# Cross attention of a hybrid decoder layer: another order of the first head's products, scores among the last head's products, two PSUM banks for transposes and values spread over the steps

## The chip, the cores and the metric

The kernel runs on one core of a Trainium2 chip. A core has a matrix engine (TensorE, PE in the profile, with its weight loads as PEld), VectorE (DVE), ScalarE (ACT), GpSimd (POOL) and SyncE (SP, which here issues loads). Each engine works through its own list of instructions and is tied to the others by semaphores. The metric is the time of one execution on the device in microseconds (us), lower is better, as the median of three runs: 1311.14 us before, from 1310.99 to 1311.16.

## The reference, cut to what matters

One decoder layer of width 1024 on 1024 tokens, in float32: token mixing (gated linear attention beside a sliding window attention, with one output projection), cross attention into 256 memory tokens, and a gated MLP with a short causal convolution. All of the change lies in the cross attention:

```python
D_MODEL, SEQ, MEM_LEN, CROSS_HEADS, CROSS_DH = 1024, 1024, 256, 4, 256

def cross_attn(h, memn, w_q, w_k, w_v, w_o):
    B, T, _ = h.shape
    q = (h @ w_q).reshape(B, T, CROSS_HEADS, CROSS_DH)
    k = (memn @ w_k).reshape(B, MEM_LEN, CROSS_HEADS, CROSS_DH)
    v = (memn @ w_v).reshape(B, MEM_LEN, CROSS_HEADS, CROSS_DH)
    s = jnp.einsum('bqhd,bkhd->bhqk', q, k).astype(jnp.float32) * (CROSS_DH ** -0.5)
    p = jax.nn.softmax(s, axis=-1).astype(v.dtype)
    o = jnp.einsum('bhqk,bkhd->bqhd', p, v).reshape(B, T, D_MODEL)
    return o @ w_o

    # in the layer, after token mixing:
    h = h + cross_attn(rms_norm(h, norm_cross[l]), rms_norm(mem, norm_mem[l]), w_q_c[l], w_k_c[l], w_v_c[l], w_o_c[l])
```

k and v of all heads are made earlier in the program and lie in device memory.

## The kernel before, in words

**Numbers.** Every float32 operand of a matmul is split in two: `hi`, a cast by ACT to the matrix engine's own format (line 110), and `lo`, the float32 value less `hi`, by DVE (line 111). A product is then three matmuls, hi·hi, hi·lo and lo·hi, added up in a PSUM bank (`mm3`, lines 149 to 151, or the inner loop at line 1273). A matmul here is 128x512 (weights 128x128, 512 columns) or, in the scores, 128x256.

**Queries.** The q of one head (256 columns, 1024 tokens, depth 1024) is made by `query_pair` as a 2x2 block product with seven products in place of eight (Winograd's form of Strassen's): products 1 to 7, each of 4x3 matmuls, with sums of input blocks (`s1` to `s4` of the activations, from `query_sums` and `mix_out`; `w1` to `w4` of the weights, from `block_weights`) and sums of the results. Products 2, 7 and 3 go on adding in the bank of another product (2 in 1's, 7 in 6's, 3 in 5's), after that bank has been read. `v1`, `u2` and `u3` are SBUF tiles for the sums (lines 1276, 1280, 1282, 1262). The heads come in the order 2, 3, 0, 1; the first one (head 2) takes the products in the order 1276543, the others 1627543. The q of heads 2 and 3 goes to device memory (`q_d`) and comes back later (`reload`), since SBUF has no room. After head 2's products `cross_scales` makes the row scales of the softmax (with a matmul against ones, `psO<-ones,ss`). The PSUM banks have roles: F and S with three banks each, T and O with one each.

**Attention.** `scores(h, g)` is 12 matmuls of 128x256 into a bank S, for a group g of 256 queries (g from 0 to 3); `softmax` takes the maximum (DVE, line 1318), two exponentials with their sums (ACT, line 1323), a reciprocal and two scalings (DVE, lines 1325, 1327). `transposed(h, g)` turns the probabilities round with four matmuls into the bank T (line 1379), and ACT and DVE split them into `pt`. `values(h, n)` are 12 matmuls for each d of 0 and 1, for half the queries n, into banks F or S, and ACT copies the results out (line 1392). In `cross` the loop over h = 0, 1, 2 and g takes a transpose of head h, the scores of head h+1 and, at g = 2 and at the next head's g = 0, a whole `values`. Then come head 3's transposes and values among the first two columns of the output projection (`out_first`, plain products) and then the other columns as seven-product pairs (`out_pair`, from line 1529 on).

**What sets the order.** On the matrix engine the order is that of the code (`manual_schedule`). On DVE, ACT, POOL and SP the framework's scheduler sets the order, and pools of tiles with a few buffers each (`st` with 3, `w`, `sx` with 12, `kv` with 4, `pt` with 4, `cp` with 3, `c` with 3) set when a tile is free again. The loads are issued by SP in order; `kv` holds k and v of a head as the matmuls want them (512 KB a tile), and its slots lie over memory that the queries used before.

## Time and profile before

| what | value |
|---|---|
| time, median of three runs | 1311.14 us (1310.99 to 1311.16) |
| time of the profiled execution | 1310.63 us |
| its span in the trace | 1308.6 us |
| granted TensorE clock, mean | 0.998 |
| PE busy | 1280.2 us, 98% |
| DVE busy | 995.3 us, 76% |
| ACT busy | 634.3 us, 48% |
| first product of the first head on PE | 424.88 us |
| first product of `out_pair` on PE | 595.89 us |

Times within the trace are counted from the start of the span. In a row of the timeline the first number is the start, the second the duration; then come engine, line, operation, output and inputs by the program's names, the shape, and in brackets the idle time ahead with what ended it. A row of the waits names the engine and line that waited, what it waited for, the sum, the count and the longest. Of the 28 us in which PE was not busy over the whole span, 14.4 us are waits on other engines or loads between 420 and 660 us.

### The profile page before, as it was taken

The numbers are of one execution on the slowest core, as the hardware profiler recorded it, in microseconds if no ns is written. First come the engines' busy times: TensorE is split into PE (matmuls) and PEld (weight loads), VectorE is DVE, ScalarE is ACT, GpSimd is POOL, SyncE is SP. The second block draws the span as 40 slices with busy tenths as digits, with TensorE's granted clock in tenths as the row PEclk, the third lists the DMA queues.
The fourth block names the chain that finished last, engine by engine and source line by source line (L and its number), as shares of the span: only waits on it lengthen the run. The fifth ranks groups of instructions, "written<-read, shape, count | busy, mean of one in ns | idle before, by whom it ended". The sixth has DMA issues, their size and how long they took to land.

```text
span 1308.6 us, 17378 instructions
## 1 busy us (share of the span) xinstructions
PE 1280.2 (98%) x6503; PEld 1067.9 (82%) x6503; DVE 995.3 (76%) x1705; ACT 634.3 (48%) x1129; POOL 103.4 (8%) x181
## 2 busy tenths in 40 slices
PE   8999999999999999799999999999999999999997
PEld 8887777989888778778888888888888888888886
DVE  6849763378556976688689988888888886999687
ACT  5525545345444534674456534443444444454455
POOL 1400111101221000001100000000000000000001
PEclk9999999999999999999999999999999999999999
DMA  7642111249843443305422333232223138710204
GB/s 222 187 115 65 62 57 61 65 141 304 215 147 105 152 146 132 126 33 193 121 74 71 122 129 97 81 97 82 77 83 97 65 109 315 284 65 9 73 17 153
DMA packets 142363, 155.30 MB, mean 119 GB/s; under 512 B 16081, under 2 KB 108422, under 8 KB 142278
## 3 DMA queue, kind: packets, MB, share of 16 engines
q1 hardware_dynamic: 128822, 111.02, 27.4%
q0 software_dynamic: 13296, 42.91, 9.3%
q8 instruction: 51, 0.84, 0.3%
q14 instruction: 34, 0.28, 0.1%
q10 hardware_dynamic: 160, 0.27, 0.1%
HBM read 113.26 MB, written 42.48 MB: 119 GB/s over the span
## 4 chain that ended last, share of the span: by engine, by line
PE 94%; DVE 3%; ACT 1%; DMA 1%; issue 0%; SPq 0%; DVEq 0%; ACTq 0%
PE psS L1752 15%; PE psF L1752 13%; PE psF L149 8%; PE psF L150 8%; PE psF L151 8%; PE psF L1867 6%; PE psS L1867 6%; PE psS L1529 3%; PE psF L1273 3%; PE psS L151 2%; PE psS L150 2%; PE psS L149 2%; PE psO L1867 2%; PE psT L1867 2%; PE psS L1273 2%; PE psO L149 2%
## 5 line engine op out<-in xcount | busy, mean ns | idle before, releaser
L110 ACT CAST w<-st 128x1024 fp32r<-128x1024 f32 (+1 forms) x148 | 126.8, 860 | 212.2 <-PE psS L1867 39.6
L111 DVE TENSOR_TENSOR w<-st,w 128x1024 fp32r<-128x1024 f32 (+1 forms) x148 | 145.3, 984 | 46.1 <-ACT w L110 46.1
L1781 DVE SCALAR_TENSOR_TENSOR uy<-uy,vec,uy 128x1023 f32<-128x1023 f32 (+1 forms) x88 | 112.2, 1279 | 1.9 <-ACT uy L1779 1.5
L1867 PE MATMUL psF<-w,w 128*128 128x512 f32 x318 | 89.0, 389 | 0.0
L1867 PE MATMUL psS<-w,w 128*128 128x512 f32 x312 | 87.5, 389 | 0.0
L1752 PE MATMUL psS<-a,w 128*128 128x512 f32 x360 | 86.5, 389 | 0.0
L149 PE MATMUL psF<-xh,w 128*128 128x512 f32 x208 | 83.0, 399 | 0.0
L151 PE MATMUL psF<-xh,w 128*128 128x512 f32 x208 | 81.5, 392 | 0.0
L150 PE MATMUL psF<-xl,w 128*128 128x512 f32 x208 | 81.2, 390 | 0.0
L1752 PEld LDWEIGHTS psS<-a,w 128*128 128x128 f32 x360 | 67.6, 188 | 14.0
L1752 PE MATMUL psF<-a,w 128*128 128x512 f32 x324 | 77.8, 389 | 0.0
L1752 PEld LDWEIGHTS psF<-a,w 128*128 128x128 f32 x324 | 60.8, 188 | 12.6
L1867 PEld LDWEIGHTS psF<-w,w 128*128 128x128 f32 x318 | 59.7, 188 | 12.4
L1867 PEld LDWEIGHTS psS<-w,w 128*128 128x128 f32 x312 | 58.6, 188 | 12.1
L1779 ACT ACTIVATE uy<-uy,vec 128x1024 f32<-128x1024 f32 x44 | 54.7, 1247 | 18.6 <-DVE uy L1772 18.3
L1752 PE MATMUL psS<-act,wx 128*128 128x512 f32 x240 | 57.6, 389 | 0.0
L1752 PE MATMUL psS<-act,w 128*128 128x512 f32 x240 | 57.6, 389 | 0.0
L1752 PEld LDWEIGHTS psS<-act,w 128*128 128x128 f32 x240 | 45.1, 188 | 9.3
L1752 PEld LDWEIGHTS psS<-act,wx 128*128 128x128 f32 x240 | 45.0, 188 | 9.4
L1752 PE MATMUL psF<-act,wx 128*128 128x512 f32 x216 | 51.9, 389 | 0.0
L1752 PE MATMUL psF<-act,w 128*128 128x512 f32 x216 | 51.9, 389 | 0.0
L1033 ACT ACTIVATE prob<-prob,nm 128x256 f32<-128x256 f32 (+1 forms) x64 | 30.9, 484 | 39.8 <-DVE nm L1029 39.7
(530 smaller groups left out, 3137.9 us busy)
## 6 DMA issues: line engine op xcount, KB each, us to landing
st<-in_w_up_dram SPq DMA_DIRECT2D x44, 512.0 KB, 3.9
g_d<-uy POOLq DMA_DIRECT2D x22, 512.0 KB, 2.9
act<-in_w_down_dram SPq DMA_DIRECT2D x12, 512.0 KB, 10.3
st<-g_d SPq DMA_DIRECT2D x10, 512.0 KB, 3.9
res<-g_d SPq DMA_DIRECT2D x10, 512.0 KB, 9.1
st<-in_w_in_dram SPq DMA_DIRECT2D x9, 512.0 KB, 6.8
xt_d<-pts POOLq DMA_DIRECT2D x16, 256.0 KB, 5.1
ow_d<-pts POOLq DMA_DIRECT2D x32, 128.0 KB, 2.7
```

Of the source, the lines that this page charges most:

```text
L110: h = nc.scalar.copy(out=hi, in_=src)
L111: l = nc.vector.tensor_tensor(out=lo, in0=src, in1=hi.bitcast(F32), op=ALU.subtract)
L149: mm(out, lhsT=lh, rhs=rh, start=start, stop=False)
L150: mm(out, lhsT=lh, rhs=rl, start=False, stop=False)
L151: mm(out, lhsT=ll, rhs=rh, start=False, stop=stop)
L1033: last = nc.scalar.activation(out=prob[:, n, :nk], in_=prob[:, n, :nk], func=AF.Exp, bias=nm[:, n:n + 1], accum_out=den[:, n:n + 1])
L1273: mm(ps[n], lhsT=left[n][l][:, q], rhs=right[n][q][r], start=new and q == 0 and i == 0, stop=new and q == 3 and i == 2, skip_group_check=n ...
L1529: mm(ps, lhsT=left[n][l][:, q], rhs=right[n][q][r], start=new and q == 0 and i == 0, stop=new and q == 3 and i == 2, skip_group_check=not new)
L1752: nc.tensor.matmul(ps, lhsT=b[l][:, q], rhs=a[q][r], start=first and q == 0 and n == 0, stop=first and q == 3 and n == 2, skip_group_check ...
L1779: nc.scalar.activation(out=y, in_=u, func=AF.Identity, scale=self.v("cw2", j), bias=self.v("conv_b", j))
L1781: nc.vector.scalar_tensor_tensor(out=y[:, s:], in0=u[:, :T - s], scalar=self.v(nm, j), in1=y[:, s:], op0=ALU.mult, op1=ALU.add)
L1867: nc.tensor.matmul(ps[i], lhsT=g[:, l, tk], rhs=w[:, r], start=first and k == 0 and m == 0, stop=first and k == n - 1 and m == 2, skip_gro ...
```

## The change

It is confined to the cross attention; the number of matmuls stays.

1. **First head (head 2).** The product order becomes 1472563, with products 1, 4, 7 in banks F and 5, 6 in banks S; product 5's bank is copied to `u3` by ACT (one instruction more), and the sums that need 6 and 7 are made behind product 6. The other heads keep 1627543, all with banks F (head 3 had S).
2. **Sums of the first head.** `query_sums` is now a generator: the splits of s1, s2, s4 are written down one after each of the first products, with all their tiles taken at once. Head 2's `b22` lies in a tile of the pool that later holds head 0's k (`kt`), and its weights' sums t1, t4 come ahead of t2, t3. Head 0's k is loaded after head 2's products.
3. **First scores.** The scores and the softmax of head 0's groups 0, 1, 2 stand among head 1's products (behind 2, 5 and 3), no longer between head 0's products and head 1's.
4. **Transposes** take the banks T and O by turns. In the loop's first round the transposes of groups 0 and 1 stand close together with the last scores of head 0 between them.
5. **Values** are spread: each `values(h, n)` gives its d = 0 to one step and its d = 1 to the next, six matmuls each, behind the scores. Head 1 takes its groups in the order 2, 3, 0, 1.
6. **Loads and homes.** The `kv` loads go in the order v0, k1, v1, k2 and then q of heads 2 and 3 (before: k1, v0, q of head 2, v1, k2, q of head 3), so the tiles take other places.
7. **The end.** Head 3's transposes and values and the products of `out_first` are in another order, and one of its products goes to bank O.

```diff
     def query_sums(self, new):
-        for n, at, sl in (("s2", 0, slice(512, 1024)), ("s1", 4, slice(512, 1024)), ("s4", 4, slice(0, 512))):
+        tiles = {n: [[new("sx", [P, 2, 512], F32R, 12) for _ in range(2)] for _ in range(2)] for n in ("s2", "s1", "s4")}
+        for n, at, sl in (("s1", 4, slice(512, 1024)), ("s2", 0, slice(512, 1024)), ("s4", 4, slice(0, 512))):
             self.qa[n] = []
             for q in range(0, 4, 2):
-                hi, lo = (new("sx", [P, 2, 512], F32R, 12) for _ in range(2))
+                hi, lo = tiles[n][q // 2]
...
+            yield
...
             elif n == "6":
                 tt(out=u2, in0=ps[n], in1=v1, op=add)
                 if first:
-                    tt(out=u3, in0=ps["7"], in1=u2, op=add)
+                    tt(out=v1, in0=ps["7"], in1=u2, op=add)
+                    summed(1, t1, u3, v1, u3)
+                    summed(0, t1, ps["4"], v1, v1)
             elif n == "7" and not first:
                 tt(out=u3, in0=ps[n], in1=v1, op=add)
+            elif n == "5" and first:
+                nc.scalar.copy(out=u3, in_=ps[n])
...
+            next(between, None)
         return out
...
+        def first_scores():
+            yield
+            for g in range(3):
+                yield
+                probs[0, g] = self.softmax(self.scores(q[0], kt, g), g, cpnew)
+                yield
+
         for n, h in enumerate((2, 3, 0, 1)):
-            order = "1276543" if n == 0 else "1627543"
-            banks = dict(zip("14567", "FFSFF" if n == 0 else "SSSS" if n == 1 else "FFFF"))
-            ready = weights
-            q[h] = self.query_pair(ready, order, banks, tmp, o8)
+            order, banks = ("1472563", "14756") if n == 0 else ("1627543", "1654")
+            q[h] = self.query_pair(weights, order, dict(zip(banks, "FFFSS" if n == 0 else "FFFF")), tmp, o8,
+                                   sums if n == 0 else first_scores() if h == 1 else iter(()))
             if n < 3:
                 weights = self.query_weights((2, 3, 0, 1)[n + 1], new)
             if n == 0:
+                kt = self.memory_load(self.k_d[0], keep())
                 self.cross_scales()
...
-            if h == 0:
-                probs = {(0, g): self.softmax(self.scores(q[0], kt, g), g, cpnew) for g in range(3)}
...
-            pt = self.bank("T").rearrange("p (k q) -> p k q", k=2)
+            pt = self.bank("TO"[g % 2]).rearrange("p (k q) -> p k q", k=2)
...
-        def values(h, n, role):
+        def values(h, n, role, ds=(0, 1)):
...
+        def turn(h, i):
+
+            return (2, 3, 0, 1)[i] if h == 1 else i
+
...
+        memory_values(0)
         keys(1)
-        memory_values(0)
-        reload(2)
         memory_values(1)
         keys(2)
+        reload(2)
         reload(3)
...
-            for g in range(4):
-                transposed(h, g)
-                if h == g == 0:
+            for i in range(4):
+                if h or i != 1:
+                    transposed(h, turn(h, i))
+                if h == i == 0:
                     probs[0, 3] = self.softmax(self.scores(q[0], kts[0], 3), 3, cpnew)
-                score = self.scores(q[h + 1], kts[h + 1], g)
-                if g == 0 and h:
-                    values(h - 1, 1, "F")
+                    transposed(0, 1)
+                score = self.scores(q[h + 1], kts[h + 1], turn(h + 1, i))
+                if h:
+                    part = (h - 1, turn(h - 1, 2) // 2) if i < 2 else (h, turn(h, 0) // 2)
+                    values(*part, "F", (i % 2,))
+                elif i > 1:
+                    values(0, 0, "F", (i - 2,))
...
         transposed(3, 0)
-        values(2, 1, "F")
+        values(2, 1, "F", (0,))
+        steps(early, 1)
+        transposed(3, 1)
+        values(2, 1, "F", (1,))
+        steps(early, 3)
+        next(first)
+        transposed(3, 2)
+        values(3, 0, "S")
+        weights = self.out_weights(1, new)
+        next(weights)
+        marks = transposed(3, 3)
         steps(early, 2)
         next(first)
...
-                banks[c, h] = self.bank("F")
+                banks[c, h] = self.bank("O" if c == h == 1 else "F")
```

The line numbers of the changed kernel are 2 to 23 higher here (1276 is 1278, 1323 is 1330, 1379 is 1393, 1392 is 1406).

**ACT in the attention's loop, around the transposes of groups 2 and 3 of head 0 and group 0 of head 1** (`pt<-psT` or `psO` is the first half of a transpose's split, 1323 or 1330 the exponentials, 1392 or 1406 a copy of values). Before:

```order
377 L110 CAST pt_5061<-psT_5063 128x2x256
378 L1323 ACTIVATE cp_5054,cden_5055<-psS_5038,cmx_5051,rs_4468 128x256 x2
379 L1392 COPY o_5083<-psF_5085 128x512
380 L110 CAST act_5487<-o_5083 128x512
381 L1392 COPY o_5084<-psF_5093 128x512
382 L1323 ACTIVATE cp_5104,cden_5105<-psS_5070,cmx_5101,rs_4468 128x256 x2
383 L110 CAST pt_5061<-psT_5111 128x2x256
384 L110 CAST act_5487<-o_5084 128x512
385 L110 CAST pt_5141<-psT_5143 128x2x256
```

The changed kernel at the same place:

```order
378 L110 CAST pt_5061<-psT_5063 128x2x256
379 L1330 ACTIVATE cp_5054,cden_5055<-psS_5038,cmx_5051,rs_4468 128x256 x2
380 L1406 COPY o_5083<-psF_5085 128x512
381 L1330 ACTIVATE cp_5096,cden_5097<-psS_5070,cmx_5093,rs_4468 128x256 x2
382 L110 CAST pt_5061<-psO_5103 128x2x256
383 L110 CAST act_5487<-o_5083 128x512
384 L1406 COPY o_5084<-psF_5123 128x512
385 L110 CAST pt_5141<-psT_5143 128x2x256
```

Each transpose's cast still stands behind a copy or a pair of exponentials, but one in two of them now reads bank O, and one copy of values stands between two casts where two stood.

**DVE in the second head of the queries (head 3)**, around the read of product 6's bank (`c_4501<-ps…_4517`, `u2` and what frees the bank for product 7; `w_…` are low halves of weights; `rs_…` are row scales). Before:

```order
606 L111 TENSOR_TENSOR wx_4461<-st_4445,wx_4460 128x1024
607 L188 TENSOR_TENSOR rs_t_4481<-rs_y_4482 128x8
608 L111 TENSOR_TENSOR w_4465<-st_4444,w_4464 128x1024
609 L189 TENSOR_TENSOR rs_t_4481<-rs_t_4481,rs_v_4480 128x8
610 L190 TENSOR_SCALAR rs_t_4481<-rs_t_4481 128x8
611 L111 TENSOR_TENSOR w_4610<-st_4605,w_4609 128x1024
612 L191 TENSOR_TENSOR rstd_4479<-rs_y_4482,rs_t_4481 128x8
613 L1280 TENSOR_TENSOR c_4501<-psS_4517,c_4500 128x512
```

The changed kernel:

```order
606 L111 TENSOR_TENSOR w_4463<-st_4442,w_4462 128x1024
607 L183 TENSOR_SCALAR rs_v_4480<-psO_4470 128x8
608 L111 TENSOR_TENSOR w_4614<-st_4606,w_4613 128x512
609 L188 TENSOR_TENSOR rs_t_4481<-rs_y_4482 128x8
610 L111 TENSOR_TENSOR w_4610<-st_4605,w_4609 128x1024
611 L189 TENSOR_TENSOR rs_t_4481<-rs_t_4481,rs_v_4480 128x8
612 L1282 TENSOR_TENSOR c_4501<-psF_4517,c_4500 128x512
```

The read of the bank now stands behind a low half (`w_4614`, row 608) of the second weight tile (`st_4606`) of the head after, too.

**DVE at the end of the loop**, around the last two transposes of head 3 (`pt<-psT`, and in the changed kernel `psO`; line 1177 and `act`, `kv` are the output projection's operands). Before:

```order
762 L111 TENSOR_TENSOR act_5626<-o_5083,act_5625 128x512
763 L111 TENSOR_TENSOR act_5626<-o_5084,act_5625 128x512
764 L1177 TENSOR_TENSOR o_5423<-o_5423,o_5083 128x512
765 L1177 TENSOR_TENSOR o_5424<-o_5424,o_5084 128x512
766 L111 TENSOR_TENSOR pt_5597<-psT_5598,pt_5596 128x2x256
767 L111 TENSOR_TENSOR kv_5634<-o_5423,kv_5633 128x512
768 L111 TENSOR_TENSOR kv_5634<-o_5424,kv_5633 128x512
769 L111 TENSOR_TENSOR act_5660<-o_5578,act_5659 128x512
770 L111 TENSOR_TENSOR act_5660<-o_5579,act_5659 128x512
771 L111 TENSOR_TENSOR pt_5597<-psT_5652,pt_5596 128x2x256
```

The changed kernel:

```order
756 L111 TENSOR_TENSOR act_5610<-o_5245,act_5609 128x512
757 L111 TENSOR_TENSOR act_5610<-o_5246,act_5609 128x512
758 L111 TENSOR_TENSOR pt_5566<-psT_5567,pt_5565 128x2x256
759 L1177 TENSOR_TENSOR o_5083<-o_5423,o_5083 128x512
760 L1177 TENSOR_TENSOR o_5084<-o_5424,o_5084 128x512
761 L1177 TENSOR_TENSOR o_5423<-o_5083 128x512
762 L1177 TENSOR_TENSOR o_5424<-o_5084 128x512
763 L111 TENSOR_TENSOR pt_5566<-psO_5600,pt_5565 128x2x256
```

Both of the last transposes' low halves now stand eight rows earlier in DVE's list, and the last one ahead of the halves of `act` and `kv` that stood between the two.

More of the change, by code (lines that the diff above doesn't have):

```diff
@@ L1236, in query_sums, with query_weights, query_pair @@
                     self.qa[n].append((hi[:, i], lo[:, i]))
-    def query_weights(self, h, new):
+            yield
+    def query_weights(self, h, new, b22=None):
         def halves():
+            if b22 is not None:
+                return iter([b22[:, s].rearrange("p d m -> p (d m)").rearrange("p (k c) -> p k c", c=P)
+                             for s in range(2)])
             return iter([new("w2", [P, 4, P], F32R, 4) for _ in range(2)])
-        _, _, weights = self.block_weights(self.a["w_q_c"][0], 2 * h * P, (2 * h + 1) * P, new, halves)
+        _, _, weights = self.block_weights(self.a["w_q_c"][0], 2 * h * P, (2 * h + 1) * P, new, halves, b22 is not None)
         return weights
-    def query_pair(self, weights, order, banks, tmp, o8):
+    def query_pair(self, weights, order, banks, tmp, o8, between=iter(())):
         nc, mm = self.nc, self.nc.tensor.matmul
@@ L1251, in query_pair @@
         left = dict(zip("1234567", (b11, b21, b22, w4, w1, w2, w3)))
-        right = dict(zip("1234567", (self.qa[n] for n in ("a11", "a12", "s4", "a22", "s1", "s2", "s3"))))
+        right = dict(zip("1234567", ("a11", "a12", "s4", "a22", "s1", "s2", "s3")))
         out = [[o8("o8", dt=F32R, bufs=8) for _ in range(2)] for _ in range(2)]
@@ L1255, in query_pair @@
         v1, u2, u3 = (tmp("c", [P, 512], bufs=3) for _ in range(3))
-        ps, first = {}, order == "1276543"
+        ps, first = {}, order[1] == "4"
         def put(d, sl, src):
@@ L1265, in query_pair @@
         for n in order:
-            new = n in "1456" or (first and n == "7")
-            if new:
-                ps[n] = self.bank(banks[n])
-            else:
-                ps[n] = ps[{"2": "1", "7": "6", "3": "5"}[n]]
+            new = n in banks
+            ps[n] = self.bank(banks[n]) if new else ps[{"2": "1", "7": "6", "3": "5"}[n]]
             for q in range(4):
                 for i, (l, r) in enumerate(((0, 0), (0, 1), (1, 0))):
-                    mm(ps[n], lhsT=left[n][l][:, q], rhs=right[n][q][r], start=new and q == 0 and i == 0,
+                    mm(ps[n], lhsT=left[n][l][:, q], rhs=self.qa[right[n]][q][r], start=new and q == 0 and i == 0,
                        stop=new and q == 3 and i == 2, skip_group_check=not new)
@@ L1381, in transposed @@
             return self.split(pt, *(t[:, :, sl] for t in parts[h, g // 2]))
-        def values(h, n, role):
-            if n == 0:
+        def values(h, n, role, ds=(0, 1)):
+            if len(self.oc) == 2 * h:
                 self.oc += [o8("o8", bufs=8) for _ in range(2)]
-            pth, ptl = parts.pop((h, n))
-            for d in range(2):
+            pth, ptl = parts[h, n]
+            for d in ds:
                 ps = self.bank(role)
@@ L1418, in cross @@
                         keys(3)
-                if g == 2:
-                    values(h, 0, "F")
-                probs[h + 1, g] = self.softmax(score, g, cpnew)
-                if h == 2 and g:
+                probs[h + 1, turn(h + 1, i)] = self.softmax(score, turn(h + 1, i), cpnew)
+                if h == 2 and i:
                     steps(early, 1)
@@ L1425, in cross @@
         transposed(3, 0)
-        values(2, 1, "F")
+        values(2, 1, "F", (0,))
[9 more added lines that the diff above has]
+        marks = transposed(3, 3)
         steps(early, 2)
         next(first)
-        transposed(3, 1)
-        steps(early, 2)
-        next(first)
-        values(3, 0, "S")
-        transposed(3, 2)
-        weights = self.out_weights(1, new)
-        next(weights)
-        steps(early, 4)
-        next(first)
-        marks = transposed(3, 3)
         for _ in early:
@@ L1444, in cross @@
         late = late()
+        next(first)
         next(first)
@@ L2126, in run @@
             o8 = o8s.enter_context(self.pool("o8"))
+            heads = ExitStack()
+            kvnew = heads.enter_context(self.pool("kv0"))
             with self.pool("p3") as new:
```

23 lines of the change are left out of this document (11 added, 12 removed).

## The prediction

> **What bounds the kernel now.** The page's busy times come first, then what the matrix engine (PE) waits for from the first head's first product (424.88 us) to the first product of `out_pair` (595.89 us), the stretch in which its order changes.
>
> ```profile
> PE 1280.2 (98%) x6503; PEld 1067.9 (82%) x6503; DVE 995.3 (76%) x1705; ACT 634.3 (48%) x1129; POOL 103.4 (8%) x181
> ...
> PEclk9999999999999999999999999999999999999999
> ```
>
> ```profile
> PE psT L1379 <- DVE pt L111: 6.1, 4, 1.5
> PE psT L1379 <- DVE cmx L1319: 2.1, 1, 2.1
> PE psF L1273 <- ACT c L1276: 1.9, 1, 1.9
> PE psS L149 <- DMA kv<-k_d: 1.5, 1, 1.5
> PE psS L149 <- ACT o L110: 1.1, 1, 1.1
> PE psS L149 <- ACT pt L110: 0.7, 1, 0.7
> PE psS L1273 <- DVE c L1262: 0.6, 1, 0.6
> PE psS L151 <- DVE o L111: 0.2, 1, 0.2
> PE psS L150 <- DVE pt L111: 0.2, 1, 0.2
> ```
>
> PE is the bound: 98% busy at full clock, so only what PE stands still, or does, counts. The list holds 12 waits, 14.4 us in all, of the 28.4 that the span has over PE's busy time. The change removes no matmul, so its gain lies in these 14.4 us and in what they hide at their edges.
>
> The five waits at line 1379 are the largest part: a transpose waits for its PSUM bank T. One such turn, on three engines:
>
> ```profile
> 524.37 0.60 PE L1379 MATMUL psT<-ident,cp 128*128 128x128 f32 x4
> 524.73 0.36 PE L149 MATMUL psS<-kv,o 128*128 128x256 f32 x1
> ...
> 526.00 0.28 PE L150 MATMUL psS<-kv,o 128*128 128x256 f32 x1
> 526.12 0.28 PE L151 MATMUL psS<-kv,o 128*128 128x256 f32 x1
> 527.93 0.63 PE L1379 MATMUL psT<-ident,cp 128*128 128x128 f32 x4 [1.53 <-DVE pt L111]
> ```
>
> ```profile
> 525.05 0.57 ACT L1323 ACTIVATE cp<-psS,cmx,rs 128x256 f32<-128x256 f32 x1
> ...
> 526.15 0.59 ACT L110 CAST pt<-psT 128x512 fp32r<-128x512 f32 x1
> ```
>
> ```profile
> 527.10 0.68 DVE L111 TENSOR_TENSOR pt<-psT,pt 128x512 fp32r<-128x512 f32 x1
> ```
>
> Bank T is written at 524.37; ACT runs a softmax's exponentials first and reads the bank at 526.15, DVE subtracts at 527.10, and the next transpose starts at 527.93, 3.56 us after the one before. PE has only a transpose (0.36) and a score (to 526.24) between. The engine that is late is not full, as the windows of heads 1 and 2 of the loop show (PE, PEld, DVE, ACT, POOL busy, clock, DMA share, GB/s):
>
> ```profile
> 540.80:560.20 19.40, 15.40 (x105) 13.75 (x103) 15.27 (x37) 14.49 (x38) 0.00 (x0) 1.00 0.09 28
> 560.20:582.00 21.80, 19.76 (x93) 15.97 (x94) 20.08 (x37) 15.07 (x30) 0.00 (x0) 1.00 0.13 49
> ```
>
> DVE is busy for 15.27 of 19.40 us, then for 20.08 of 21.80: the first stretch is latency, the second is close to a throughput limit.
>
> **The price of a wait.** The last score matmul before the wait started at 526.12 and the one before it at 526.00: the pitch is 0.12 at a duration of 0.28, so the next could have started at 526.24. It started at 527.93, 1.69 us later, where the list counts 1.53. Each of the 12 waits thus costs some 0.16 more than listed, 1.9 in all: **16.3 us** is what they cost.
>
> A second way to the same number is the content of the stretch:
>
> ```profile
> 424.88 2.88 PE L1273 MATMUL psF<-act,w 128*128 128x512 f32 x12
> ...
> 435.42 2.89 PE L1273 MATMUL psF<-sx,wx 128*128 128x512 f32 x12
> 438.14 2.88 PE L1273 MATMUL psS<-sx,w 128*128 128x512 f32 x12
> ...
> 447.54 1.84 PE L223 MATMUL psO<-ones,ss 128*128 128x1 f32 x16
> ...
> 529.84 0.40 PE L149 MATMUL psF<-pt,kv 128*128 128x512 f32 x1
> ...
> 532.59 0.60 PE L1379 MATMUL psT<-ident,cp 128*128 128x128 f32 x4
> ...
> 595.89 3.11 PE L1529 MATMUL psS<-act,w 128*128 128x512 f32 x13
> ```
>
> A product takes 438.14 − 435.42 = 2.72, two half values 532.59 − 529.84 = 2.75, a score 1.51, a transpose 0.36, the scales 1.7. With 28 products (76.2), 16 scores (24.2), 16 transposes (5.8), 16 half values (22.0), the eight products of `out_first` (21.8), the scales and five matmuls of `out_pair` (1.1) that is 152.8 of 595.89 − 424.88 = 171.0. So 18.2 us is not content; the 1.9 beside the 16.3 are starts some 0.1 us late behind a semaphore, which stay.
>
> **The transposes** (two banks, values spread): a step of the loop is now a transpose, a score and a half of values, 0.36 + 1.51 + 1.375 = 3.25 us, and a bank is asked for again after two steps, 6.5 us, against the 3.56 it takes to come free. The 6.1 and 2.1 us and five edges go: 9.0. What hides the cycle is the other bank and the half of values in each step; with one bank and the steps even, 3.56 − 3.25 would be left, 0.3 a step. In the first round, with a score between the first two transposes and none of values, T is asked for again after 0.36 + 1.51 + 0.36 + 2 × 1.51 = 5.25. DVE must now keep up in the round h = 2.
>
> ```profile
> 433.45 1.22 DVE L111 TENSOR_TENSOR w<-st,w 128x1024 fp32r<-128x1024 f32 x1
> 434.58 3.09 DVE L111 TENSOR_TENSOR sx<-o,sx 128x512 fp32r<-128x512 f32 x5
> ```
>
> Five rows at 512 columns took 3.09, 0.60 apart; one at 1024 columns is followed after 1.13. From the round's first transpose to the last of head 3 DVE has 33 rows at 512 columns (19.8) and the small ones of five softmaxes (by estimate 3.6): 23.4 us, against 25.5 of PE, 92%. That is the tightest place.
>
> **The first head.**
>
> ```profile
> 429.65 3.03 PE L1273 MATMUL psF<-act,w 128*128 128x512 f32 x12 [1.89 <-ACT c L1276]
> ```
>
> ```profile
> 427.46 1.65 ACT L110 CAST sx<-o 128x512 fp32r<-128x512 f32 x3
> 429.02 0.57 ACT L1276 COPY c<-psF 128x512 f32<-128x512 f32 x1
> ```
>
> Product 2 waits until product 1's bank is copied, and the copy stands behind three casts though product 1 ended at 427.76. In the new order 4 and 7 stand between 1 and 2, in banks of their own, 5.4 us of cover; product 3 adds on in 5's bank behind product 6, 2.72 of cover for ACT's copy. The waits of 1.9 and of 0.6 (the list's row at 1273 on DVE `c`) go, with edges 2.8. New: product 4, second in the order, needs the last block (`a22`) at about 429.7, three matmuls before its end. ACT has two casts of weights in front of that block's scaling; with the pitches of the rows I get the last low half at 429.7: between 0 and 0.5, taken as 0.05. The sums s1, s2, s4 I get at 433.7, 436.1, 438.5, for needs at 435.8, 438.5, 441.2: 2 us of room, no wait.
>
> **The second head** (head 3) is where the new order of DVE can cost. Product 7 adds on in 6's bank once DVE has read it into `u2`.
>
> ```profile
> 451.94 0.37 SPq L1715 DMA_DIRECT2D st<-in_w_q_c_dram  x1
> ```
>
> ```profile
> 457.40 0.63 ACT L110 CAST w<-st 128x512 fp32r<-128x512 f32 x1 [3.61 <-DMA st<-in_w_q_c_dram]
> ```
>
> ```profile
> 455.04 0.69 DVE L1280 TENSOR_TENSOR c<-psS,c 128x512 f32<-128x512 f32 x1
> ```
>
> That read now stands behind a low half of a weight tile of the head after (row 608 of DVE's order). Its load is issued once its staging tile is free, by my walk of DVE's rows (1.13 at 1024 columns, 0.60 at 512) at 445.1, and took 5.4 us before (451.94 to 457.3): 450.5, then a cast (0.63), the halves (0.60 and 1.13) and the small rows, so `u2` is read by 453.2 to 454.8. Head 3's product 7 is due at 445.62 + 3 × 2.72 = 453.8, a wait of 0 to 1.0, or 1.6 if DVE comes late to it. I take 0.5.
>
> **Loads, first scores, the end.** The first row is a window while the loads run, at 399 GB/s.
>
> ```profile
> 514.80:516.80 2.00, 0.62 (x5) 0.65 (x6) 1.12 (x3) 0.73 (x3) 0.00 (x0) 1.00 1.00 399
> ```
>
> ```profile
> 512.81 0.34 SPq L1302 DMA_DIRECT2D kv<-k_d  x1
> ```
>
> ```profile
> 516.18 0.35 PE L149 MATMUL psS<-kv,o 128*128 128x256 f32 x1 [1.53 <-DMA kv<-k_d]
> ...
> 577.72 0.51 PE L149 MATMUL psS<-pt,kv 128*128 128x512 f32 x1 [0.67 <-ACT pt L110]
> ```
>
> k of head 1 is issued at 512.81, when the last product frees its slot, and used at 516.18: 3.4 us, and PE had a transpose and a score of work. Now v of head 0 goes first, into a slot that is free a product earlier; k still waits for the last product, behind which PE has the score of group 2, a transpose, a score and a transpose ahead of the score that needs it: 1.51 + 0.36 + 1.51 + 0.36 = 3.7 against 3.4. The wait goes (1.7 with its edge); 0 to 1.5 may be left if v0's transfer ahead of it slows it, and I take 0.05. The first scores stood straight behind head 0's products and waited for their last sums (1.1 + 0.2, with edges 1.6); among head 1's products they have at least three products of cover. At the end the 0.7 and 0.2 (1.2 with edges) go, but `values(3, 1)` comes some 3.1 us after its last transpose, where the bank cycle above is 3.4 to 3.6: 0.4 is left, between 0 and 0.9.
>
> **Sum.** 9.0 + 2.8 + 1.7 + 1.6 + 1.2 = 16.3 removed; 0.05 + 0.5 + 0.05 + 0.4 = 1.0 new: 15.3 gained. All behind 595.89 depends on `out_pair`'s start and PE's rows there have no gap, so it stays. The profiled execution took 1310.63 for a span of 1308.6, about 2.0 outside it, and lies 0.5 below the median of the runs, 1311.14. The span becomes 1293.3, the median **1295.8 us**. With no new wait and the late starts halved it is 1294; with every bound of a new wait at its upper end (0.5 + 1.6 + 1.5 + 0.9 = 4.5) 1299.3. The likeliest case's own range is 1293.3 to 1297.8.
>
> **The rivals.**
>
> *A: the followers become the bound.* What fell away on PE was slack for DVE and ACT, whose lists run in order: a low half that waits for its weights holds every later read of a bank. For it: `u2` above, the 92% of the round h = 2, and 20.08 of 21.80 us in the window. Against: the first window's 79%. The price, at twice what I took in each of three places (1.0 in head 3, 1.0 at the end) and 2 us where DVE, at 23.4 plus 10% for its semaphores, passes PE's 25.5: 4 us, 1299. [...]
>
> *B: the loads come late.* q of head 2 now queues behind four tiles of k and v. k of head 1 lands 3.4 us after the last product, and the last tile of q of head 2 is the sixth behind it, each 512 KB at 399 GB/s, 1.31 us: 3.4 + 6 × 1.31 = 11.3. It is needed after six scores, five transposes and two half values, 13.6. For a delay: k and v still wait for slots, in order on SP, so one late slot holds all behind it. If k of head 1 is 1.5 late and q 3, the time is 1300. Against: two microseconds of room.
>
> *C: no gain.* The waits are the throughput of ACT and DVE in the loop and only move. Then 9.0 comes back and the new waits reach their upper 4.5: 2.8 is left of the 16.3, 1308.3, and within 0.2% of 1311.14 as soon as one more wait of half a microsecond stays. Against: 79% of DVE in the window where most waits lie.
>
> *D: slower.* One mechanism: PE without pauses from 424 us on gets less clock. For it: nothing yet; the clock is 1.00 in all windows above and 9 tenths or more in all 40 slices. It decides from a mean clock of 1293.3 / 1308.6 = 0.988 for the whole span; at 0.97, 1293.3 / 0.97 + 2.5 = 1336. [...]
>
> **How the numbers follow.** Forecast 0.62, A 0.20, B 0.10, C 0.04, D 0.04. The range has to take in A's and B's lower halves: 1293 to 1301 holds nearly all of the forecast's case and most of A and B, 0.8 or a little more. About 0.2%, 2.6 us, is what a measurement here tells from no change: faster by more 0.92, within it 0.04, slower by more 0.04.
>
> **What would show it.** In the new profile: no wait at the transposes (the list's first two rows gone; if T's wait goes and O's comes, two banks weren't enough); the first head's products 2.72 apart from 424.88 to 443.9; in head 3 a wait of at most 1 us before product 7, released by DVE `c`; no wait for `kv<-k_d` over 0.3; the first `out_pair` product at 580 to 582; the clock at 1.00. A wait over 2 us anywhere in 424 to 582, or PE idle behind 582, would make the forecast wrong, as would a busy time of DVE in the round h = 2 over 24 us.

## The result and the profile after

The changed kernel takes 1292.91 us (median), against 1311.15 for the kernel before in the same session: a ratio of 0.9857, 95% interval 0.9837 to 0.9876. One of the changed kernel's four executions took 5808.45 us; the ratio compares the means without it, and the other three lie between 1292.56 and 1293.01. The change gains 18.2 us, 1.4%; 15.3 were forecast, and the time lies 0.1 us below the lower end of the range.

The page's busy times of the changed kernel, and all waits of PE over its whole span:

```profile
PE 1277.1 (99%) x6503; PEld 1067.9 (83%) x6503; DVE 993.5 (77%) x1705; ACT 633.1 (49%) x1130; POOL 103.4 (8%) x181
```

```profile
PE psO L260 <- DMA vrows<-in_norm_mix_dram: 3.2, 1, 3.2
PE psS L521 <- DMA gr<-in_x_dram: 1.2, 1, 1.2
PE psF L149 <- ACT w L113: 0.8, 1, 0.8
PE psS L1013 <- DVE mx L1022: 0.2, 1, 0.2
```

All four rows belong to the work ahead of the cross attention. Between 420 and 650 us the list is empty: the twelve waits of before are gone and none took their place. The matrix engine's timeline in the attention:

```profile
425.18 5.60 PE L1275 MATMUL psF<-act,w 128*128 128x512 f32 x24
430.62 2.88 PE L1275 MATMUL psF<-act,wx 128*128 128x512 f32 x12
...
444.22 1.84 PE L223 MATMUL psO<-ones,ss 128*128 128x1 f32 x16
...
507.49 0.60 PE L1393 MATMUL psT<-ident,cp 128*128 128x128 f32 x4
...
519.17 0.60 PE L1393 MATMUL psT<-ident,cp 128*128 128x128 f32 x4
...
522.44 0.60 PE L1393 MATMUL psO<-ident,cp 128*128 128x128 f32 x4
...
545.23 0.60 PE L1393 MATMUL psT<-ident,cp 128*128 128x128 f32 x4
...
577.07 4.24 PE L1552 MATMUL psS<-act,w 128*128 128x512 f32 x18
```

The first two products stand in one row of 24 matmuls without a gap, a step of the loop takes 522.44 − 519.17 = 3.27 us (3.25 forecast), and `out_pair` starts 577.07 − 425.18 = 151.9 us after the first product, where it took 171.0. The content that the prediction counted was 152.8 with five matmuls (1.1) that now stand behind this point: 151.7. The stretch is at its content.

**A ruler for the runs.** The time ahead of the first product differs from execution to execution by up to 2 us (423.5 to 425.5 us in the fourteen traces here, also between kernels whose work there is alike). So the parts are measured in the trace from the first product's start to the end of the span, which leaves that out: 1308.6 − 424.9 = 883.7 us before, 1290.8 − 425.2 = 865.6 us after, 18.1 us less. The changed kernel and the two variants of it without any wait there (e7 and e8 below) differ by 0.1 us on this ruler. Each kernel has one trace, though, and a load that lands late in it counts as a loss (e4 below).

### The profile page after: what moved, and what is told of

Its sections match the earlier page's. It is cut to its first block, busy times and chain, and to the rows that moved or that the text cites. A ratio compares the mean times of both kernels' runs of the same rounds, so it can differ in the third digit from the quotient of the medians.

```text
span 1290.8 us, 17377 instructions
## 1 busy us (share of the span) xinstructions
PE 1277.1 (99%) x6503; PEld 1067.9 (83%) x6503; DVE 993.5 (77%) x1705; ACT 633.1 (49%) x1130; POOL 103.4 (8%) x181
## 4 chain that ended last, share of the span: by engine, by line
PE 98%; ACT 1%; DVE 0%; DMA 0%; issue 0%; SPq 0%; ACTq 0%; DVEq 0%
PE psS L1775 15%; PE psF L1775 13%; PE psF L149 8%; PE psF L150 8%; PE psF L151 8%; PE psF L1890 6%; PE psS L1890 6%; PE psF L1275 5%; PE psS L1552 3%; PE psS L149 3%; PE psS L150 3%; PE psS L151 3%; PE psO L1890 2%; PE psT L1890 2%; PE psO L149 2%; PE psO L151 2%
## 5 line engine op out<-in xcount | busy, mean ns | idle before, releaser
L1804 DVE SCALAR_TENSOR_TENSOR uy<-uy,vec,uy 128x1023 f32<-128x1023 f32 (+1 forms) x88 | 112.0, 1278 | 1.9 <-ACT uy L1802 1.5
```

Source lines behind the costliest of these rows:

```text
L1804: nc.vector.scalar_tensor_tensor(out=y[:, s:], in0=u[:, :T - s], scalar=self.v(nm, j), in1=y[:, s:], op0=ALU.mult, op1=ALU.add)
```

## The experiments

| kernel | first product, us | span, us | first product to end, us | against | difference, us | time, us | ratio to before, 95% interval |
|---|---|---|---|---|---|---|---|
| before | 424.88 | 1308.6 | 883.69 | | | 1311.15 | |
| changed | 425.18 | 1290.8 | 865.59 | before | −18.10 | 1292.91 | 0.9857 [0.9837, 0.9876] |
| e1, one bank | 424.11 | 1292.0 | 867.90 | changed | +2.31 | 1294.41 | 0.9864 [0.9849, 0.9878] |
| e2, values whole | 425.31 | 1292.6 | 867.30 | changed | +1.71 | 1294.08 | 0.9861 [0.9847, 0.9876] |
| e3, both of these | 424.50 | 1299.5 | 874.99 | changed | +9.40 | 1301.63 | 0.9919 [0.9904, 0.9934] |
| e4, before with two banks | 425.47 | 1303.0 | 877.49 | before | −6.20 | 1303.46 | 0.9931 [0.9914, 0.9947] |
| e5, first head's old order | 423.90 | 1295.4 | 871.47 | changed | +5.88 | 1297.72 | 0.9898 [0.9881, 0.9914] |
| e6, first scores back | 424.99 | 1293.9 | 868.89 | changed | +3.30 | 1295.82 | 0.9880 [0.9865, 0.9895] |
| e7, old order of loads | 423.50 | 1289.1 | 865.65 | changed | +0.06 | 1291.97 | 0.9852 [0.9837, 0.9866] |
| e8, more work on DVE | 424.79 | 1290.4 | 865.66 | changed | +0.07 | 1291.91 | 0.9851 [0.9836, 0.9866] |
| e9, before with the new first head | 425.07 | 1305.1 | 880.02 | before | −3.67 | 1306.59 | 0.9967 [0.9954, 0.9980] |
| e12, old end | 424.48 | 1291.7 | 867.25 | changed | +1.66 | 1293.82 | 0.9868 [0.9852, 0.9885] |
| e10, longer wait | 423.96 | 1309.2 | 885.27 | before | +1.58 | 1311.27 | one run |
| e11, much longer wait | 424.82 | 1321.6 | 896.74 | before | +13.05 | 1323.63 | one run |

The kernels were measured in several sessions, in which the kernel before took 1311.15 (changed, e5 to e8), 1312.30 (e1 to e4) and 1311.30 us (e9 to e12). By their times alone e1, e2, e6 and e12 can't be told from the changed kernel, since their intervals overlap its own; what is said of them rests on the traces. The spans of e7 and e8 are 1.7 and 0.4 us shorter than that of the changed kernel, and their first products came 1.7 and 0.4 us earlier (423.50 and 424.79); on the ruler they are equal.

### Two banks or values spread: e1 to e4

```diff
# e1, on the changed kernel (e4 is the reverse, on the kernel before)
-            pt = self.bank("TO"[g % 2]).rearrange("p (k q) -> p k q", k=2)
+            pt = self.bank("T").rearrange("p (k q) -> p k q", k=2)
# e2, on the changed kernel; e3 is e1 and e2 together
-                if h:
-                    part = (h - 1, turn(h - 1, 2) // 2) if i < 2 else (h, turn(h, 0) // 2)
-                    values(*part, "F", (i % 2,))
-                elif i > 1:
-                    values(0, 0, "F", (i - 2,))
+                if h and i == 0:
+                    values(h - 1, turn(h - 1, 2) // 2, "F")
+                elif i == 2:
+                    values(h, turn(h, 0) // 2, "F")
...
-        values(2, 1, "F", (0,))
+        values(2, 1, "F")
         steps(early, 1)
         transposed(3, 1)
-        values(2, 1, "F", (1,))
```

> The changed kernel with one difference: all transposes go to bank T again, values stay spread. Theory S (the cycle of the bank is latency, and even steps alone nearly cover it): in the changed kernel's trace a transpose's bank was free 2.0 to 3.5 us after the transpose's start, and a step takes 3.25 us, so only the short gaps wait: 0.3 and 0.2 in head 1's round, about 1 at the first pair of transposes (1.87 us apart), 0.4 at head 3's first pair (1.82 apart); with edges +2 to +3 us, 1295 to 1296. Theory B (the second bank is the cure): the waits of before come back, five of 1.5 to 2.1 or more, +8 to +10 us, 1301 to 1303.

> The changed kernel with one difference: the values stand whole (12 matmuls) in one step, as before, two banks stay. Theory B (two banks are enough): a bank is asked for again after two steps, 6.5 us however the values are spread, so no wait comes back: 0 to +1 us, 1293 to 1294. Theory S (the spread is the cure): steps without values are 1.87 us and ACT and DVE have only that between two transposes, so waits of about 1 us at every second step, +4 to +6 us, 1297 to 1299.

> The changed kernel with both undone: one bank T and whole values. Both theories: the five waits at the transposes of before come back and one more at the first pair, 9 to 11 us, 1302 to 1304. A third theory, that the waits came from the old order of ACT and DVE and not from the bank, expects less than half of that, under 1297.

> The kernel before with one difference: transposes take banks T and O by turns. Theory B: the five waits at the transposes go, 8.2 listed and 9.0 to 9.8 with their edges: 1301.5 to 1302.5. Theory S: two banks without the spread only move the waits to the probabilities' scaling or to the scores, less than 5 us is gained: 1306 or more.

The two theories were put as if one edit were the cure. Each nearly is, by itself. With one bank and the values spread, 2.31 us are lost; two of its transposes, and the list's only row:

```profile
PE psT L1393 <- DVE pt L111: 0.7, 3, 0.3
```

```profile
519.22 0.63 PE L1393 MATMUL psT<-ident,cp 128*128 128x128 f32 x4 [0.25 <-DVE pt L111]
522.51 0.60 PE L1393 MATMUL psT<-ident,cp 128*128 128x128 f32 x4
526.06 0.63 PE L1393 MATMUL psT<-ident,cp 128*128 128x128 f32 x4
```

Steps of 3.29 and 3.55 us: the bank's cycle shows through at 3.55, the 3.56 that the prediction had read from one turn, and it took 0.2 to 0.5 us in six places. The list names three of them. The transpose at 526.06 is 0.3 us late and has no bracket: the matmul ahead of it hides 0.16 of that with its tail (its duration of 0.39 over a pitch of 0.23), and the 0.14 that is left is less than any wait in these lists.

With two banks and whole values the loop has no wait at all. The 1.71 us of e2 stand around one row, at the loop's end, where a whole `values` follows head 3's first transpose with no score between:

```profile
547.52 0.50 PE L150 MATMUL psF<-pt,kv 128*128 128x512 f32 x1 [1.25 <-DVE pt L111]
```

With neither, the waits of before are back, and one more (9.40 us):

```profile
PE psT L1393 <- DVE pt L111: 6.3, 5, 1.5
PE psT L1393 <- DVE cmx L1326: 2.0, 1, 2.0
```

So the two edits replace each other: alone the spread is worth 9.40 − 2.31 = 7.1 us, the second bank 9.40 − 1.71 = 7.7, both 9.4. On the kernel before (e4) the second bank took away all five waits, yet the trace shows only 6.2, for others came. Of these rows one wait of 0.6 was there before, and the largest new one stands at the same place as in e2:

```profile
PE psS L1273 <- DVE c L1262: 1.2, 2, 0.6
PE psF L150 <- DVE pt L111: 1.1, 1, 1.1
PE psF L1273 <- DVE o L111: 0.2, 1, 0.2
```

By the trace's parts the second bank brought 8.8 us from the loop's first transpose to head 3's first, about what the theory of the bank expected, and lost 1.5 behind that and 1.0 in the first two heads, far from the transposes. The wait of 0.2 lies in the first head, at product 4, which starts 0.2 us late in the kernel before too, without a row. The second wait of 0.6 lies in the second head, where DVE's rows stand in the order of before, but a load of weights landed 1.0 us later. DVE's row behind that load, before and in e4:

```profile
457.40 0.69 DVE L1728 TENSOR_TENSOR st<-st,st 128x512 f32<-128x512 f32 x1 [1.52 <-DMA st<-in_w_q_c_dram]
```

```profile
459.08 0.69 DVE L1728 TENSOR_TENSOR st<-st,st 128x512 f32<-128x512 f32 x1 [2.54 <-DMA st<-in_w_q_c_dram]
```

Whether this belongs to e4 or to this one execution is not shown; the traced execution took 1304.99 us, the other three 1302.81 to 1303.79. The 6.2 is thus a lower value, and nearer 7 without the late load. Of the theories, neither "spread alone" nor "bank alone" stands for the whole kernel; the bank's cycle does.

### The first head's products: e5 and e9

```diff
# e5, on the changed kernel
-        for n, at, sl in (("s1", 4, slice(512, 1024)), ("s2", 0, slice(512, 1024)), ("s4", 4, slice(0, 512))):
+        for n, at, sl in (("s2", 0, slice(512, 1024)), ("s1", 4, slice(512, 1024)), ("s4", 4, slice(0, 512))):
...
                 if first:
-                    tt(out=v1, in0=ps["7"], in1=u2, op=add)
-                    summed(1, t1, u3, v1, u3)
-                    summed(0, t1, ps["4"], v1, v1)
+                    tt(out=u3, in0=ps["7"], in1=u2, op=add)
...
-            order, banks = ("1472563", "14756") if n == 0 else ("1627543", "1654")
+            order, banks = ("1276543", "17654") if n == 0 else ("1627543", "1654")
...
# e9: the changed kernel with cross() of before, out_first's old banks, and the first scores behind head 0's products
```

> The changed kernel with one difference: the first head's products in the order 1276543 again, with the old banks, sums and order of the splits. The prediction's term: the waits of 1.9 and 0.6 come back, 2.8 with their edges: 1295.5 to 1296. If the splits of the sums, which are now written in one after another, were the larger help, the old waits would not come back in full: under +1.5.

> The kernel before with the first two parts of the change alone (order and banks of the first head's products, its sums and its weights' homes, head 0's k loaded later); scores, transposes, values, loads and the end are as before. The prediction's term: the waits of 1.9 and 0.6 go, 2.8 with edges: from the first product to the end 883.69 - 2.8 = 880.9 us in the trace. If the two waits undone in the changed kernel (5.9 us there) are the measure, 877.8. If the second head's wait for `u2` exists in this surrounding, 881.4.

The old order in the new surroundings (e5) cost 5.88 us, twice the forecast. PE's row of the second product, and windows around it (PE, PEld, DVE, ACT, POOL busy, granted clock, DMA share, GB/s):

```profile
430.15 4.60 PE L1275 MATMUL psF<-act,w 128*128 128x512 f32 x12 [3.36 <-ACT c L1278]
```

```profile
427.00:431.50 4.50, 1.35 (x4) 1.14 (x5) 4.50 (x9) 4.50 (x10) 0.00 (x0) 0.91 0.40 117
431.50:434.00 2.50, 2.50 (x7) 1.95 (x6) 2.50 (x6) 2.50 (x6) 0.00 (x0) 0.50 0.00 0
434.00:437.00 3.00, 3.00 (x14) 2.41 (x14) 3.00 (x6) 1.37 (x3) 0.00 (x0) 0.98 0.00 0
```

Two things are in it. The wait for ACT's copy is 3.36 us and not 1.89, since ACT's list now has three casts of weights (423.88, 424.84 and 428.48 us) between the first product's start and that copy, where the kernel before has none; the new order had been covering that as well. And behind the wait the granted clock is 0.50 (in the window of 2.5 us above, and for 3.4 us in all): the product takes 4.60 us for 2.88. Undoing a part is thus not the same as the part by itself. By itself, on the kernel before (e9), the new first head is worth 3.67 us, 0.9 over the forecast. The waits at its products are gone, and from the first product to the matmul of the scales it takes 19.04 us where it took 22.66, 3.62 less. PE's wait for k of head 1 (1.5) is gone too, as its home was free early (issued at 501.09), but a transpose two steps on now waits in its place, so that this exchange is worth next to nothing:

```profile
516.15 0.66 PE L1388 MATMUL psT<-ident,cp 128*128 128x128 f32 x4 [1.40 <-DVE pt L111]
```

### First scores and loads: e6 and e7

```diff
# e6, on the changed kernel
...
-                                   sums if n == 0 else first_scores() if h == 1 else iter(()))
+                                   sums if n == 0 else iter(()))
...
+            if h == 0:
+                probs = {(0, g): self.softmax(self.scores(q[0], kt, g), g, cpnew) for g in range(3)}
# e7, on the changed kernel
-        memory_values(0)
         keys(1)
+        memory_values(0)
+        reload(2)
         memory_values(1)
         keys(2)
-        reload(2)
         reload(3)
```

> The changed kernel with one difference: the first three scores stand between head 0's and head 1's products again. Both theories: the waits on ACT and DVE `o` come back, 1.3 listed, 1.6 with edges. Theory K (the wait for k of head 1 went because a score now stands behind the last product): k is issued at the last product's end, lands 3.4 us later, and PE has 0.36 + 1.51 + 0.36 = 2.2 ahead of it: 1.2 more, in all +3 us, 1295.5 to 1296.5. Theory L (it went because of the order of the loads): +1.6 alone, 1294.5.

> The changed kernel with one difference: k and v and the reloaded q in the old order (k1, v0, q of head 2, v1, k2, q of head 3), and with it other homes. Theory K: no wait comes back, within 0.3 of the changed kernel, 1292.6 to 1293.2. Theory L: the wait for k of head 1 comes back, +1.5 to +1.8, 1294.5.

Both came out as theory K had it. With the scores put back, PE waits for ACT and DVE and, 27 us later, for the load again; with the loads put back, for nothing:

```profile
PE psS L149 <- DMA kv<-k_d: 1.2, 1, 1.2
PE psS L149 <- ACT o L110: 1.1, 1, 1.1
PE psS L151 <- DVE o L111: 0.2, 1, 0.2
```

The 1.2 us is what the sum of 3.4 (landing) less 2.2 (work ahead) had given. In the new order of loads the score that moved behind the last product is the load's cover. The old order is worth as much (0.06 us), but it does not need that cover: in e7 k of head 1 gets the home that is free early and is issued at 494.72 (506.02 in the changed kernel), as in e9, where the wait went without the score. So e7 does not show that the homes have no weight.

### DVE full, and PE not waiting: e8

```diff
-        nc.vector.tensor_reduce(out=mx, in_=ps, axis=mybir.AxisListType.X, op=ALU.max)
+        for _ in range(1 + more):     # more is 1 for the scores of head 3, 0 elsewhere
+            nc.vector.tensor_reduce(out=mx, in_=ps, axis=mybir.AxisListType.X, op=ALU.max)
...
```

> The changed kernel with four more maxima on DVE (each written twice, the same result), one per group of the loop's round h = 2, 0.60 us each, 2.4 us. DVE is busy for 22.35 of 22.63 us there and 22.24 of 22.24 us in the stretch behind. Theory bound (rival A of the prediction): PE waits for what is added, +1.5 to +2.5 us, 1294.5 to 1295.5. Theory slack (DVE works ahead there on operands of the output projection that are needed later): 0 to +0.5 us, 1293 to 1293.5.

The window of the round h = 2, first of the changed kernel, then of e8:

```profile
532.20:554.83 22.63, 22.63 (x138) 19.72 (x137) 22.35 (x52) 20.32 (x49) 0.00 (x0) 1.00 0.06 22
```

```profile
532.20:554.83 22.63, 22.63 (x139) 19.72 (x137) 22.49 (x53) 19.52 (x47) 0.00 (x0) 1.00 0.05 19
```

DVE is busy for 99% of the round in both, and 2.4 us of additional work cost 0.07. Part of what fills DVE there, 6.4 us in the changed kernel, are low halves for the output projection (`act`), which are wanted later: ten such rows stand in its window and eight in that of e8, so the added maxima pushed some of them back, and PE did not wait. Rival A read the share of busy time as nearness to a limit, and that falls.

### The end: e12

The edit puts the text from `first = self.out_first(...)` to the end of `cross` back, with product (1, 1) in bank F.

> The changed kernel with one difference: from head 3's first transpose on (transposes, last values, products of `out_first`, banks) the old order. The prediction's term: the waits of 0.7 and 0.2 come back, 1.2 with edges: from the first product to the end 865.59 + 1.2 = 866.8 us. The rest of the 18.1 us that the other undone parts leave (18.1 - 9.4 - 3.3 - 2.8 to 3.1 = 2.3 to 2.6) would make it 868.

It cost 1.66 us, between the two numbers. PE's rows at head 3's first values:

```profile
560.91 0.50 PE L149 MATMUL psS<-pt,kv 128*128 128x512 f32 x1 [0.68 <-ACT pt L110]
561.68 0.50 PE L150 MATMUL psS<-pt,kv 128*128 128x512 f32 x1 [0.27 <-DVE pt L111]
```

**The parts, added up.** Transposes 9.40 (e3), first head 3.67 (e9), first scores 3.30 (e6), loads 0.06 (e7), end 1.66 (e12): 18.09 us, where the whole change measured 18.10. That it closes to 0.01 is luck. e3 holds a wait of 0.2 at the first pair of transposes that the kernel before does not have, e6 has 1.2 for k's load where before has 1.5, and with the first head's 5.88 of e5 in place of the 3.67 of e9 the sum would be 20.3. So the first head's part depends on what stands around it, as the two halves of the first part (e1, e2) do on one another.

The two traces give the parts without any experiment. These rows are of the kernel before:

```profile
447.54 1.84 PE L223 MATMUL psO<-ones,ss 128*128 128x1 f32 x16
...
512.61 0.60 PE L1379 MATMUL psT<-ident,cp 128*128 128x128 f32 x4
...
561.34 0.63 PE L1379 MATMUL psT<-ident,cp 128*128 128x128 f32 x4 [1.53 <-DVE pt L111]
```

From the first product to the scales the change gains 3.62 us, from there to the first transpose 1.80, from that to head 3's first transpose 10.99, from there to `out_pair` 1.58 (the five matmuls counted alike) and behind it 0.11.

### What a longer wait costs: e10 and e11

```diff
# on the kernel before; 3 in e10, 5 in e11
             if n == "1":
-                nc.scalar.copy(out=v1, in_=ps[n])
+                for _ in range(3 if first else 1):
+                    nc.scalar.copy(out=v1, in_=ps[n])
```

> The kernel before with ACT's copy of the first head's product 1 written three times, so that PE's wait of 1.9 us there becomes 2.9. If only a stall as long as 3.4 us brings the clock down (as in the kernel with the first head's old order), the time from the first product to the end grows by 1.0 us and no more, the product behind the wait takes 3.0 us. If every stall beyond the 2.1 us that the kernel before had does, it grows by 2.5 and the granted clock behind the wait is about 0.5.

> The kernel before with the same copy written five times: a wait of 4 to 6 us (two casts come in between). If a stall over 3.4 us halves the granted clock for some 3.4 us, the next 8 or so matmuls take 0.63 us and the time grows by the added wait and 1.4 to 1.7 us on top; if the drop in the other kernel came from something else there, by the added wait alone.

e10 has the wait, 3.12 us, and the drop, which one of the two expectations allowed only at 3.4 us:

```profile
429.97 4.61 PE L1273 MATMUL psF<-act,w 128*128 128x512 f32 x12 [3.12 <-ACT c L1277]
```

```profile
427.00:429.00 2.00, 0.00 (x0) 0.00 (x0) 2.00 (x5) 1.97 (x5) 0.00 (x0) 1.00 0.19 41
429.00:431.00 2.00, 1.03 (x3) 0.82 (x4) 2.00 (x5) 1.93 (x4) 0.00 (x0) 0.87 0.65 231
431.00:433.00 2.00, 2.00 (x6) 1.61 (x5) 2.00 (x3) 1.99 (x3) 0.00 (x0) 0.50 0.00 0
433.00:435.00 2.00, 2.00 (x8) 1.60 (x8) 2.00 (x4) 0.39 (x1) 0.00 (x0) 0.78 0.54 147
```

The product takes 4.61 us where it took 3.03. Of the added 1.2 + 1.6 us 1.4 are left at the end of the first head, since the wait of 0.6 and the late starts there were absorbed; 0.18 more were lost at k's load, 1.58 in all. In e11 the wait was 10.19 us where 4 to 6 were expected, since the last two copies came behind other casts (433.75 and 437.25 us). The clock was 0.50 from 430.0 until 443.7 us, and it fell twice more, at 563.1 and 573.4 us, behind these waits:

```profile
562.62 0.63 PE L1380 MATMUL psT<-ident,cp 128*128 128x128 f32 x4 [2.08 <-DVE cmx L1320]
...
572.72 0.63 PE L1380 MATMUL psT<-ident,cp 128*128 128x128 f32 x4 [1.88 <-DVE pt L111]
```

The 13.05 us that e11 lost are 9.58 in the first head, 1.89 at the first and 1.59 at the second of these drops. The first of the two is the wait of 2.1 us that the kernel before has too, without a drop there. Why it drops the clock in one trace and not in the other is read from the traces in the last section.

## Why the prediction was right or wrong

**The bound and the mechanism: right.** The matrix engine's waits between 424 and 596 us were the gain, all twelve of them. The second way to the number, content against the stretch's length, gave 18.2 us of which 18.1 were gained. The sum went by the first way, and came out 2.8 us too low: `out_pair` started at 577.07, ahead of the 580 to 582 named as a sign. That the time lies only 0.1 us below the range is due to the range's lower end, which allowed for the case that no new wait comes and half of the late starts go; no new wait came, and nearly all of the late starts went.

**The step that failed is the price of a wait**, "Each of the 12 waits thus costs some 0.16 more than listed, 1.9 in all", with the sentence on the starts "which stay". Listed 14.4, gained 18.1: the list was short by 3.7 us and not by 1.9, 0.31 per wait on average. The experiments give the same order with other waits: e12 lists 0.95 in two waits and costs 1.66 (0.36 each over the list), e6 2.5 in three and 3.30 (0.26 each), e3 8.3 in six and 9.40 (0.18 each, transposes). The 0.16 is the tail of the matmul ahead (0.28 us over a pitch of 0.12).

Part of what was left out stands in a row that the prediction quotes: the product behind the wait of 1.89 took 3.03 us and one without a wait 2.88. The second matmul behind a wait starts late once more, by some 0.1 us at a product or a score (behind the wait that ended at 489.01 it comes at 489.23, 0.22 us later, where the others of that score stand 0.12 apart) and 0.03 at a transpose (0.63 us where one without a wait takes 0.60); with seven waits of the one kind and five of the other that is by estimate 0.8 us. Another part are late starts that the list does not have at all, as product 4 of the first head, in the kernel before:

```profile
441.09 3.01 PE L1273 MATMUL psF<-act,w 128*128 128x512 f32 x12
```

It stands 2.95 us behind product 5 (438.14), where the pitch is 2.72, and has no bracket. So the first head, with 2.5 us listed, held 3.62 us that went: it is the term most under its size, 2.8 in the sum. So the starts did not stay: 1.8 of their 1.9 us went with the waits. About half of that is traced to rows here, the rest is not.

**The four new waits, 1.0 together: none came.** Each was set at a value between its bounds, and no wait shows for any of them in the changed kernel.

```profile
452.67 0.69 DVE L1282 TENSOR_TENSOR c<-psF,c 128x512 f32<-128x512 f32 x1
...
556.67 0.68 DVE L111 TENSOR_TENSOR pt<-psO,pt 128x512 fp32r<-128x512 f32 x1
```

```profile
454.18 2.88 PE L1275 MATMUL psF<-act,wx 128*128 128x512 f32 x12
...
554.83 0.60 PE L1393 MATMUL psO<-ident,cp 128*128 128x128 f32 x4
...
558.03 0.39 PE L149 MATMUL psS<-pt,kv 128*128 128x512 f32 x1
```

`u2` was read by 453.36, 0.8 us ahead of product 7 (0.5 had been charged). The load behind it was issued at 445.30 and cast at 449.42, so it landed within 4.1 us; the 5.4 of before were taken over from a moment with more transfers (a DMA share of 1.02 from 451.94 to 457.30 us there; here 0.26 in the first 1.7 us of the load and 0.75 from 445.30 to 449.42). The last transpose's low half was done at 557.35, 0.7 us ahead of `values(3, 1)`: 2.5 us after the transpose, not the 3.4 to 3.6 of the loop's cycle, since DVE had only four rows of line 1177 (2.4 us) ahead of it and no softmax. The late block `a22` came in time, and so did k of head 1, with next to nothing to spare: it was issued at 506.02 and used at 509.71, 3.7 us later, which is also what it took in e6, where PE waited for it (509.07 to 512.79).

**Term by term**, by the experiments: transposes 9.0 forecast, 9.40 measured; first head 2.8 and 3.67; first scores with k's load 1.6 + 1.7 = 3.3 and 3.30; end 1.2 and 1.66; new waits −1.0 and 0. The differences are 0.4 + 0.9 + 0 + 0.5 + 1.0 = 2.8 us. By the two traces they are first head 0.8, first scores 0.2, transposes with k's load 0.3 (10.7 and 10.99), end 0.4, behind `out_pair` 0.1 and new waits 1.0, again 2.8.

**The rivals.** A (DVE becomes the bound): DVE did become full, 22.35 of 22.63 us, more than the 92% forecast (23.4 of 25.5, so the sum for PE was 2.9 us too long), and e8 shows that this was no bound. That the lists run in order shows at the first head's copy of before, which started behind three casts at 429.02, 1.3 us after its bank was done (427.76); the 10% for semaphores in this rival's price was the author's estimate, and no run shows it. B (late loads): no load came late; k of head 1 needs the score ahead of it (e6) or an early home (e7, e9). C (the waits only move): fell with the empty list. D (clock): the granted clock is 0.998 in both kernels; it was waits that brought it down here (of 3.36 us in e5, 3.12 in e10, 10.19, 2.08 and 1.88 in e11) and not dense work (1.00 in the changed kernel's round h = 2, where PE is busy for all of 22.63 us).

## What to carry to other kernels

Price a gap on the matrix engine by the time from content to content and not by the list of waits: here a wait took 0.3 us more than listed on average, and late starts of 0.2 to 0.3 us were not listed at all. A charge for a wait that has not been seen needs a walk that shows it late; four halves of bounds added up to a microsecond that nobody paid. Two edits that break the same cycle, a second buffer and more work between its uses, did not add up here (7.7 and 7.1 us alone, 9.4 together), so it is worth trying each alone; and a busy share of 99% on a following engine did not make it the bound here (2.4 us of additional work cost 0.07 in e8), since part of what filled it was wanted later.

## What was unexpected in the hardware

A wait of 3.1 to 3.4 us on the matrix engine halved its granted clock (0.50) for 3.4 us and so cost 1.6 to 1.7 us on top of itself (e5, 3.36 us: a product took 4.60 us for 2.88; e10, 3.12 us: 4.61 for 3.03). In e11 waits of 2.08 and 1.88 us did the same, while the kernel before has the one of 2.09 without it.

What decides, as far as the traces show, is where the wait falls. In e11 the clock changes at 430.01, 443.67, 563.13, 566.55, 573.37 and 576.79 us, which are 4, 35, 1, 2 and 1 steps of 3.413 us apart (146.78 us for 43 of them). In the kernel before it falls at 1303.01 us, when PE's work is done, and counted back from there by 220 such steps, one ends at 552.08 us. In e11 the wait of 2.08 us lies inside one step, and the next step has the clock 0.50:

```profile
559.72:563.13 3.41, 1.33 (x12) 1.15 (x12) 3.41 (x9) 1.67 (x6) 0.00 (x0) 1.00 0.00 0
563.13:566.55 3.42, 3.42 (x17) 3.23 (x16) 2.63 (x7) 1.67 (x5) 0.00 (x0) 0.50 0.02 5
```

In the kernel before the step's end cuts the wait (551.04 to 553.13 us) in two, and each step has only 1.0 us of idle time:

```profile
548.67:552.08 3.41, 2.37 (x19) 2.04 (x17) 3.41 (x10) 3.11 (x8) 0.00 (x0) 1.00 0.00 0
552.08:555.49 3.41, 2.36 (x18) 2.32 (x19) 2.62 (x8) 1.68 (x5) 0.00 (x0) 1.00 0.02 5
```

In the fourteen traces, behind their first 14 us, the steps at the full clock with 2.08 us of idle time or more (2.84 in e5, 2.92 in e10, 2.75 ahead of 1303.01 in the kernel before) were followed by the lower clock, and those with 1.66 or less were not (the kernel before has up to 1.53); of two in between, 1.87 (e11) was and 1.89 (e4) was not. At 0.50 it was otherwise: in e11 the step from 436.84 to 440.25 us had 1.05 us of idle time and the next was at 0.50 as well; PE was busy through all of that one, and at 443.67 the clock was back at 1.00. So the kernel before was lucky with its waits of 1.9 and 2.1 us, and the same wait may cost 1.6 to 1.9 us more, as the drops of e11 did, in a kernel where other work ahead of it takes another time.
